# Hybrid decoder block on one core: where early weights are loaded and by whom, when the last row is transposed, and how early the first FFN weights are asked for

## The chip, the core and the metric

The kernel runs on one core of a Trainium2 chip. The core has a matrix engine (TensorE, "PE" in the profile, with its weight loads on the row "PEld"), a vector engine (DVE), a scalar engine (ACT), GpSimd (POOL), and SyncE (SP), which here only issues DMA transfers ("SPq" in the profile; a transfer issued by ACT is "ACTq"). On-chip data lies in SBUF, matmul results in eight PSUM banks, everything else in HBM ("DRAM"). The metric is the device time of one execution in microseconds, measured as a median over runs.

## The reference

One decoder block over x of 2048 tokens by 1024 channels, all in float32:

```
h = rmsnorm(x, g_mix_pre) * (1 + scale_m) + shift_m
q, k, v, u = split(h @ w_in)                      # 8 heads of 64, and 512 pooling channels
mix = concat(stick_breaking_attention(q, k, v), pooling_mixer(u)) @ w_out
x = x + gate_m * rmsnorm(mix, g_mix_post)
h = rmsnorm(x, g_ffn_pre) * (1 + scale_f) + shift_f
f = (silu(h @ w_gate) * (h @ w_up)) @ w_down      # 1024 -> 2816 -> 1024
x = x + gate_f * rmsnorm(f, g_ffn_post)
```

The shifts, scales and gates come from a vector c by a small product. Only the end of the mix and the FFN matter here.

## The kernel before

**Products.** A float32 product is made of three matmuls in a shorter format: each operand is split into a high part (a cast) and a low part (the rest), and hi*hi, hi*lo... are summed in a bank (`mm3`, lines 69 to 71). So whatever enters a product is first split: ACT casts (line 1173) and writes the rounded value into a PSUM bank (line 1180), DVE subtracts (line 1181). `split_by_bank` does this with the banks 6 and 7 in turn ("rounded").

**Fewer products.** The FFN's products are made by a Winograd form of Strassen's scheme: seven half-size products instead of eight, at the price of sums of operands ahead of them and sums of results behind them. For the first quarter of each matrix (`inner`) the scheme is applied once more, inside. POOL makes most operand sums: `p_s` (lines 1338 to 1344) for the inner blocks, `wd` (line 1558) for w_down, `hs` (line 1558) for the tokens, `g_s` and `u_s` (lines 1436 to 1447) for w_gate and w_up.

**The mix loop.** For 16 rows of 128 tokens PE makes the product with w_out (`mix`); `after_mix` squares it (ACT, line 1241), scales it (DVE, line 1245), which frees its bank, and adds the old x, which was loaded as `xr` (SP, line 1236; POOL, line 1247). `ffn_rows` normalizes the new row, and `put_h2` transposes it on PE (`f_pt`, line 134), scales it (`f_h`, lines 139 and 142) and stores it as operand of the FFN (`h2d`). In this loop a scheduler sets the order on every engine.

**The steps.** From the last row on, the order of PE, ACT, DVE and POOL is the written one; SP's order is still the scheduler's, which may put a transfer far ahead of its written place if its buffer is free. The work is a list of steps, one product group each. First come 22 inner blocks (q = 0 and 1, j = 0 to 10, in all m = 11q + j), each of seven steps of six matmuls, named a, e, f, b, h, i and d after their results. Then come the 11 blocks of `gate_up` for the first half of the tokens, whose first is interleaved: g(s2), the last inner block's d, g(s3), g(s1), u(s2), u(s3), u(s1) and so on, twelve matmuls each. Each step has a list `ahead` of actions that are done so many steps sooner: loads, sums. Splits are made up to six steps ahead, sums of results one step behind.

**What hangs on what.** The raw weights of an inner block (`p`, 512 KB in two loads, lines 1318 to 1326) go into one of four tiles, w320 and w321 of the pool `ring` and w320 and w321 of the pool `fx`. `fx` lies where the mix loop has its tiles and opens when the loop closes. The first tiles of gate_up (`g`, `u`, two loads of 512 KB each, line 1416) use the same four. The side tasks are put between the steps: `second_operands` (the last row's transposes and the operands of q = 1), `main_operands` (tokens for gate_up, during q = 1), `rest_operands` (`b_raw`, `t_raw`, split into `b22` and `t4`, at the entry of gate_up). `down_sums` loads four pieces of w_down (`wd`, line 1568), makes four sums on POOL six to nine steps later and stores them (`tdt`, line 1573) for the end of the kernel, 11 groups in all; its four tiles (tag "tr") are the same in each group, so a group's loads wait for the stores of the group before. `px` (line 1513) loads an inner result of 1 MB (`pd`) back for gate_up's sums.

**Banks.** The inner products use the banks 4, 2, 3, 1 and, for d and e, 5 and 0; gate_up's take 4, 2, 3, 0, 1, 5 in turn. So its g(s2) waits until the last inner h has been read from bank 4 (DVE, `u3p`, line 1390), its g(s3) until the last i has been read from bank 2 (DVE, `p_c`, line 1368), its u(s2) until the last d has been read from bank 0.

## Time and profile before

| what | value |
|---|---|
| median of 3 runs | 2243.64 us (2243.42 to 2246.16) |
| the profiled execution's own time | 2245.18 us |
| its span, first to last instruction | 2243.3 us |
| PE busy | 2204.7 us (98%) |
| DVE, ACT, POOL busy | 1604.1, 1352.3, 1301.1 us |
| mean granted PE clock | 0.996 |
| DMA | 478.13 MB, 213 GB/s over the span |

The profile is one execution. A timeline row gives start, duration, engine, line, operation and "output<-inputs"; the bracket at its end is the idle time of that engine just before, with what ended it. A wait row sums such idle times by who waited for whom. A merged row ("x4") starts at its first and lasts to the end of its last instruction. Numbers of buffers are left out of the names there; in the instruction order below they stand.

### The profile page before, as it was taken

Reading aid. Unit: us, or ns where it says so; the run is one execution under the profiler, and the core shown is the slowest. Engines: PE = TensorE matmul, PEld = TensorE weight load, DVE = VectorE, ACT = ScalarE, POOL = GpSimd, SP = SyncE. Lnnn points to the kernel's source line nnn. Section 1 sums busy time; section 2 is a strip of 40 time slices with the busy share of each in tenths; the row PEclk is TensorE's granted clock in tenths of the full one; section 3 lists DMA queues with packets and bytes.
Section 4 is the critical chain, followed back from the end, with each engine's and each line's share of the span. In section 5 each row is a group of like instructions: output and inputs, shape, how many; then the busy total and the mean of one; then the engine's idle time right before and its main releaser. Section 6 shows DMA issues by size and latency. Waiting matters only on the chain. (4 is left out here: it accounts for less than half of the span.)

```text
span 2243.3 us, 34420 instructions
## 1 busy us (share of the span) xinstructions
PE 2204.7 (98%) x10481; PEld 1824.0 (81%) x10481; DVE 1604.1 (72%) x2386; ACT 1352.3 (60%) x2752; POOL 1301.1 (58%) x1702
## 2 busy tenths in 40 slices
PE   8999999999999999999998999999999999999998
PEld 6888888888888887878887888888888888888887
DVE  7874599999999965557786565566877666555566
ACT  6335599898999844457665555545545455544444
POOL 1452277787779955538875777762314888761003
PEclk9999999999999999999999999999999999999999
DMA  9986876533443456668999566558768755548664
GB/s 316 346 280 211 283 203 182 145 109 114 118 123 104 159 177 191 211 225 278 300 336 322 180 199 191 185 190 285 236 219 277 248 192 193 191 147 311 210 189 149
DMA packets 364214, 478.13 MB, mean 213 GB/s; under 512 B 23735, under 2 KB 211707, under 8 KB 361085
## 3 DMA queue, kind: packets, MB, share of 16 engines
q1 hardware_dynamic: 361948, 472.78, 65.8%
q10 hardware_dynamic: 2080, 3.15, 0.5%
q8 instruction: 83, 1.36, 0.3%
q14 instruction: 103, 0.84, 0.1%
HBM read 323.27 MB, written 152.57 MB: 212 GB/s over the span
## 5 line engine op out<-in xcount | busy, mean ns | idle before, releaser
L952 POOL TENSOR_TENSOR w<-sg,pr 128x512 f32<-128x512 f32 (+2 forms) x320 | 306.2, 957 | 46.4 <-DVE pr L947 15.2
L947 DVE TENSOR_TENSOR_SCAN pr<-pr,carry,begin 128x512 f32<-128x512 f32 x192 | 244.0, 1271 | 0.0
L931 ACT ACTIVATE sg<-z 128x512 f32<-128x512 f32 (+2 forms) x320 | 183.8, 574 | 50.9 <-PE z L929 41.5
L60 DVE TENSOR_TENSOR wtl<-wt,wth 128x512 fp32r<-128x512 f32 (+1 forms) x320 | 189.5, 592 | 17.8 <-ACT wth L59 15.6
L59 ACT CAST wth<-wt 128x512 fp32r<-128x512 f32 (+1 forms) x320 | 183.0, 572 | 10.4 <-PE wt L963 8.1
L933 ACT ACTIVATE pr<-z 128x512 f32<-128x512 f32 (+2 forms) x320 | 183.0, 572 | 0.0
L1531 POOL TENSOR_TENSOR s<-s,cu 128x512 f32<-128x512 f32 x88 | 116.1, 1319 | 110.6 <-DVE cu L1530 105.5
L963 PE MATMUL wt<-ident,w 128*128 128x128 f32 x1088 | 172.4, 273 | 1.5 <-POOL pr L943 1.1
L963 PEld LDWEIGHTS wt<-ident,w 128*128 128x128 f32 x1088 | 134.1, 140 | 32.7 <-POOL pr L943 1.9
L1521 ACT ACTIVATE s<-s 128x512 f32<-128x512 f32 x88 | 55.6, 633 | 164.2 <-DVE s L1520 164.2
L978 PE MATMUL av<-wth,vt 128*128 128x512 f32 (+1 forms) x320 | 126.2, 394 | 0.9 <-ACT o L983 0.8
L70 PE MATMUL dn0p<-w0p_l,g0p_h 128*128 128x512 f32 x308 | 120.1, 390 | 1.3 <-DVE w0p_l L60 1.3
L71 PE MATMUL dn0p<-w0p_h,g0p_l 128*128 128x512 f32 x308 | 120.0, 390 | 0.0
L69 PE MATMUL dn0p<-w0p_h,g0p_h 128*128 128x512 f32 x308 | 120.0, 390 | 0.0
L928 PE MATMUL z<-kt,qt 128*128 128x512 f32 (+2 forms) x320 | 118.7, 371 | 0.7 <-ACT pr L933 0.6
L979 PE MATMUL av<-wtl,vt 128*128 128x512 f32 (+1 forms) x320 | 117.9, 369 | 1.3 <-DVE wtl L60 1.2
L929 PE MATMUL z<-kt,qt 128*128 128x512 f32 (+2 forms) x320 | 117.1, 366 | 0.0
L69 PE MATMUL dn1p<-w1p_h,g1p_h 128*128 128x512 f32 x292 | 113.7, 390 | 0.0
L70 PE MATMUL dn1p<-w1p_l,g1p_h 128*128 128x512 f32 x292 | 113.7, 390 | 0.0
L71 PE MATMUL dn1p<-w1p_h,g1p_l 128*128 128x512 f32 x292 | 113.7, 389 | 0.0
L1181 DVE TENSOR_TENSOR u_s_l<-u_s,rounded 128x512 fp32r<-128x512 f32 x63 | 43.3, 688 | 97.7 <-ACT rounded L1180 97.7
L944 DVE TENSOR_TENSOR_SCAN pr<-pr,zero,begin 128x128 f32<-128x128 f32 (+3 forms) x128 | 111.1, 870 | 1.7 <-ACT pr L933 1.7
(774 smaller groups left out, 7180.4 us busy)
## 6 DMA issues: line engine op xcount, KB each, us to landing
pd<-p_c SPq DMA_DIRECT2D x88, 256.0 KB, 4.5
px<-pd SPq DMA_DIRECT2D x22, 1024.0 KB, 5.7
g<-in_w_gate_dram SPq DMA_DIRECT2D x42, 512.0 KB, 4.2
u<-in_w_up_dram SPq DMA_DIRECT2D x42, 512.0 KB, 5.4
wc<-in_w_cond_dram SPq DMA_DIRECT2D x32, 512.0 KB, 7.2
qt<-qd SPq DMA_DIRECT2D x64, 256.0 KB, 4.0
kt<-kd SPq DMA_DIRECT2D x96, 128.0 KB, 3.3
vt<-vd SPq DMA_DIRECT2D x48, 256.0 KB, 3.9
```

What stands on the lines that cost most here:

```text
L59: nc.scalar.copy(hi, src)
L60: low.tensor_tensor(lo, src, raw(hi), ALU.subtract)
L69: nc.tensor.matmul(ps, lh, rh, start=first and i == 0, stop=False)
L70: nc.tensor.matmul(ps, lh, rl, start=False, stop=False)
L71: nc.tensor.matmul(ps, ll, rh, start=False, stop=last and i == n - 1)
L928: nc.tensor.matmul(z[:, 0:L], qt[:, 0, i * P:(i + 1) * P], keys, start=True, stop=False)
L931: nc.scalar.activation(sg[:, 0:L], z[:, 0:L], AF.Sigmoid, scale=0.125)
L933: nc.scalar.activation(pr[:, 0:L], z[:, 0:L], AF.Sigmoid, scale=-0.125)
L947: nc.vector.tensor_tensor_scan(keys, keys, begin, carry, ALU.mult, ALU.bypass)
L952: nc.gpsimd.tensor_tensor(w[:, 0:L], sg[:, 0:L], pr[:, 1:L + 1], ALU.mult)
L963: nc.tensor.transpose(wt[:, i * P:(i + 1) * P], wss[u][i][:, b * P:(b + 1) * P], ident)
L978: nc.tensor.matmul(av[:, lo0:], vb, wh[:, lo0:], start=first, stop=False)
```

## The change

It has six parts.

1. Inner blocks: the four weight tiles are taken in the same rotation, shifted by one block, except for the first. Block 2 is in ring w321 where it was in ring w320, block 3 in fx w320 where it was in ring w321, and so on.
2. The raw weights of the last inner block (m = 21) lie in a tile of the pool of the tokens' operands (tag "y22"), which the 1 MB tile `px_0` takes afterwards.
3. The weight loads of blocks 2 and 5 are issued by ACT, at their place in ACT's written order, instead of SP.
4. Block 0 of gate_up asks for its weights 18 and 16 steps ahead (g before: 16 and 13, u before: 14 and 10), and makes u's sums two steps sooner.
5. The last row's transposes, and the operand work behind them in the same task, come two steps later.
6. The w_down groups stand 12 steps apart instead of 13, the first two steps later (10 + 12i instead of 8 + 13i), the last so eight steps sooner.

```diff
--- before.py
+++ after.py
@@ -1316,14 +1316,17 @@
         st = {}
 
         def load():
-            turn = (2 * HF - 1 - m) % 4
+            turn = 0 if m == 1 else (2 * HF - 2 - m) % 4
             if m == 0:
                 st["g"], st["u"], st["s12"], st["s34"] = (t[:, n] for t in raw_pair(ring, name, (P, 2, TB)) for n in range(2))
             else:
-                w = raw_tile(ring if turn > 1 else fx, turn % 2 == 0, name, (P, 2, TB))
+                if m == 2 * HF - 1:
+                    w = opools["0"].tile([P, 4, TB], F32, tag="y22", bufs=1, name=f"{name}_32")
+                else:
+                    w = raw_tile(ring if turn > 1 else fx, turn % 2 == 0, name, (P, 2, TB))
                 st["g"], st["u"] = w[:, 0], w[:, 1]
             for n, src in (("g", w_gate), ("u", w_up)):
-                nc.sync.dma_start(st[n].rearrange("p (k n) -> p k n", k=HK), rows_of(src, q * HK, j))
+                (nc.scalar if m in (2, 5) else nc.sync).dma_start(st[n].rearrange("p (k n) -> p k n", k=HK), rows_of(src, q * HK, j))
 
         half = TB // 2
         one, two = slice(0, half), slice(half, TB)
@@ -1489,7 +1492,7 @@
             r.insert(0, r.pop(3))
             ahead = ((9, load_a22), (7, load0), (5, load1)) if kind == "g" else ((12, load_a22), (8, load0), (7, load1))
         elif sb == at == 0:
-            ahead = ((16, load0), (13, load1), (8, s3), (7, s2), (6, s1), (5, s4)) if kind == "g" else ((14, load0), (10, load1), (6, s3), (5, s2), (4, s1), (3, s4))
+            ahead = ((18, load0), (16, load1), (8, s3), (7, s2), (6, s1), (5, s4)) if kind == "g" else ((18, load0), (16, load1), (8, s3), (7, s2), (6, s1), (5, s4))
         elif at == 1 and kind == "g":
             ahead = ((10 if sb else 13, load0), (10 if sb else 8, load1), (6, s3), (5, s2), (4, s1), (3, s4))
         else:
@@ -1596,6 +1599,8 @@
         yield
         yield
         nxt = load(0)
+        yield
+        yield
         put_h2(*late.pop(0), fx)
         yield
         yield
@@ -1956,7 +1961,7 @@
         at[rest_operands] = len(r) - 2
         for i in range(HF):
             for n, op in zip((0, 6, 7, 8, 9), down_sums(i)):
-                r[8 + 13 * i + n].ahead.append((0, op))
+                r[10 + 12 * i + n].ahead.append((0, op))
         for sb in range(2):
             for n in range(HF):
                 s = gate_up(sb, (n - 1) % HF if sb else n, n)
```

What it does to the order of instructions is seen at three places. In these rows `p_2_...` is inner block 2 of q = 0, `p_10_...` the last of q = 1, the numbers at the end are buffers.

On SP, in the mix loop, before; xr is the old x of a row, h2d and x1d are stores of earlier rows, m, l the operands of the next products:

```order
L1282 DMA h2d_120<-f_h_11564 128x512
L1058 DMA m_11486<-mtd_98 128x4x128 x2
L1249 DMA x1d_112<-x_8_11573 128x1024
L1056 DMA l_3_11923<-mld_100 128x4x128
L1326 DMA p_2_320_13100<-in_w_gate_dram 128x4x128
L1326 DMA p_2_320_13100<-in_w_up_dram 128x4x128
L1326 DMA p_3_321_13206<-in_w_up_dram 128x4x128
L1236 DMA xr_11676<-in_x_dram 128x1024
L1058 DMA m_11486<-mtd_96 128x4x128
```

and now:

```order
L1282 DMA h2d_120<-f_h_11564 128x512
L1058 DMA m_11486<-mtd_98 128x4x128 x2
L1249 DMA x1d_112<-x_8_11573 128x1024
L1056 DMA l_3_11923<-mld_100 128x4x128
L1236 DMA xr_11676<-in_x_dram 128x1024
L1058 DMA m_11486<-mtd_96 128x4x128
```

The weights of blocks 2 and 3 (and the load of w_gate for block 3 a round earlier) have left the mix loop: block 3's come on SP after the last row of the loop, block 2's on ACT at the start of the steps.

On DVE, at the last row's transposes (f_h from f_pt), before; p_0 and p_1 are the inner blocks 0 and 1:

```order
L1181 TENSOR_TENSOR p_1_s_l<-p_1_s_13097,rounded 128x512
L1368 TENSOR_TENSOR p_0_c_13161<-bp_0_13138,p1p_0_13116 128x512
L142 TENSOR_SCALAR f_h_13172<-f_pt_13167,af,bf 128x128 x4
L1390 TENSOR_TENSOR u3p_0_13199<-hp_0_13154,u2p_0_13145 128x512
L1368 TENSOR_TENSOR p_0_c_13201<-ep_0_13103,u3p_0_13199 128x512
L1368 TENSOR_TENSOR p_0_c_13217<-ip_0_13192,u3p_0_13199 128x512
L1181 TENSOR_TENSOR p_1_s_l<-p_1_s_13118,rounded 128x512
```

and now:

```order
L1181 TENSOR_TENSOR p_1_s_l<-p_1_s_13097,rounded 128x512
L1371 TENSOR_TENSOR p_0_c_13161<-bp_0_13138,p1p_0_13116 128x512
L1393 TENSOR_TENSOR u3p_0_13177<-hp_0_13154,u2p_0_13145 128x512
L1371 TENSOR_TENSOR p_0_c_13179<-ep_0_13103,u3p_0_13177 128x512
L1371 TENSOR_TENSOR p_0_c_13195<-ip_0_13170,u3p_0_13177 128x512
L1181 TENSOR_TENSOR p_1_s_l<-p_1_s_13118,rounded 128x512
L142 TENSOR_SCALAR f_h_13208<-f_pt_13203,af,bf 128x128 x4
```

The transposed row's scaling stands four instructions later; on PE the transposes themselves stood between the products hp and ip of block 0 and now stand behind ip and block 1's ap, ahead of dp.

On POOL, at the entry of gate_up, before; wd is the last group of w_down, g_0 and u_0 the first weights of gate_up:

```order
L1344 TENSOR_TENSOR p_10_s_15526<-p_10_321_15405,p_10_s_15512 128x256
L1558 TENSOR_TENSOR wd_512_15506<-wd_512_15510,wd_512_15506 128x512
L1558 TENSOR_TENSOR wd_0_15504<-wd_512_15506,wd_0_15504 128x512
L1436 TENSOR_TENSOR g_0_s_15619<-g_0_320_15493,g_0_321_15545 128x512
L1558 TENSOR_TENSOR wd_512_15510<-wd_512_15510,wd_0_15504 128x512
L1443 TENSOR_TENSOR g_0_s_15633<-g_0_321_15545,g_0_s_15619 128x512
L1558 TENSOR_TENSOR wd_0_15508<-wd_0_15508,wd_0_15504 128x512
L1439 TENSOR_TENSOR g_0_321_15545<-g_0_321_15545 128x512
L1447 TENSOR_TENSOR g_0_s_15673<-g_0_320_15493,g_0_s_15633 128x512
L1436 TENSOR_TENSOR u_0_s_15718<-u_0_320_15587,u_0_321_15654 128x512
```

and now:

```order
L1561 TENSOR_TENSOR wd_0_15384<-wd_0_15384,wd_0_15380 128x512
L1346 TENSOR_TENSOR p_10_s_15533<-p_10_32_15419 128x256
L1347 TENSOR_TENSOR p_10_s_15533<-p_10_32_15419,p_10_s_15517 128x256
L1439 TENSOR_TENSOR g_0_s_15627<-g_0_320_15476,g_0_321_15505 128x512
L1446 TENSOR_TENSOR g_0_s_15640<-g_0_321_15505,g_0_s_15627 128x512
L1442 TENSOR_TENSOR g_0_321_15505<-g_0_321_15505 128x512
L1450 TENSOR_TENSOR g_0_s_15675<-g_0_320_15476,g_0_s_15640 128x512
L1439 TENSOR_TENSOR u_0_s_15693<-u_0_320_15536,u_0_321_15572 128x512
```

The four w_down sums stand ahead of the last of block 21's own sums, and the eight sums of gate_up's block 0 follow each other.

On SP at the same place, before; pd are stores of inner results (`p_8_c`: block 19, `p_9_c`: block 20):

```order
L1416 DMA g_0_321_15545<-in_w_gate_dram 128x8x128
L1364 DMA pd_165<-p_8_c_15524 128x512
L1364 DMA pd_164<-p_8_c_15537 128x512
L1513 DMA px_0_15617<-pd_164 128x2048
L1416 DMA u_0_320_15587<-in_w_up_dram 128x8x128
L1364 DMA pd_165<-p_8_c_15571 128x512
```

and now, in two pieces:

```order
L1419 DMA g_0_321_15505<-in_w_gate_dram 128x8x128
L1576 DMA tdt_168<-wd_512_15382 128x512
L1419 DMA u_0_320_15536<-in_w_up_dram 128x8x128
L1576 DMA tdt_167<-wd_0_15380 128x512
L1367 DMA pd_164<-p_8_c_15514 128x512
L1576 DMA tdt_166<-wd_512_15386 128x512
L1367 DMA pd_165<-p_8_c_15530 128x512
L1419 DMA u_0_321_15572<-in_w_up_dram 128x8x128
```

```order
L1419 DMA g_1_320_15723<-in_w_gate_dram 128x8x128
L1516 DMA px_0_15625<-pd_164 128x2048
L1367 DMA pd_165<-p_9_c_15685 128x512
L1659 DMA b_raw<-h2d_124 128x512
L1659 DMA b_raw<-h2d_125 128x512
```

`px_0` stood between the loads of g and u, and u's second load eight rows further down, behind three results of block 20 (`p_9_c`); now u's second load stands ahead of all of these, and `px_0` comes after them and ahead of `b_raw`.

## The prediction

> **What bounds the kernel now.** The page's first part comes first, then who waited for whom on PE from the end of the attention on, then timelines at those waits.
>
> ```profile
> PE 2204.7 (98%) x10481; PEld 1824.0 (81%) x10481; DVE 1604.1 (72%) x2386; ACT 1352.3 (60%) x2752; POOL 1301.1 (58%) x1702
> ...
> PE mix L69 <- DVE x L1245: 5.6, 4, 2.9
> PE t_g L69 <- DVE p_c L1368: 3.8, 1, 3.8
> PE t_g L69 <- DVE u3p L1390: 2.8, 1, 2.8
> PE f_pt L134 <- DVE x1s L1263: 1.9, 1, 1.9
> ...
> PE ep L69 <- ACT rounded L1180: 0.3, 1, 0.3
> ```
>
> PE is the bound: 2204.7 of 2243.3 us. The change removes no matmul, so all it can give is in PE's waits, and these are few: 5.6 us in the mix loop (four times), 1.9 + 1.0 at the last row's transposes, 2.8 + 3.8 at the entry of gate_up, 0.3 between. All lie before 1224 us; behind that the change moves nothing that PE waits for. A wait costs more than itself where the clock falls: the transposes' and the entry's rows below show products at half speed.
>
> **Part 1: weight loads leave the mix loop.** SP's timeline, the chain from its load of the old x to PE's wait of 2.9, and the landing times of all 15 such loads:
>
> ```profile
> 847.69 0.46 SPq L1326 DMA_DIRECT2D p<-in_w_gate_dram  x1
> 848.20 1.05 SPq L1326 DMA_DIRECT2D p<-in_w_up_dram  x2
> 849.35 0.44 SPq L1236 DMA_DIRECT2D xr<-in_x_dram  x1
> ...
> 856.46 1.30 POOL L1247 TENSOR_TENSOR x<-x,xr 128x512 f32<-128x512 f32 x1 [5.24 <-DMA xr<-in_x_dram]
> ...
> 860.28 1.06 ACT L1255 ACTIVATE xr<-x 128x1024 f32<-128x1024 f32 x1 [9.41 <-POOL x L1247]
> ...
> 866.48 1.41 DVE L1245 SCALAR_TENSOR_TENSOR x<-mix,mr_r,gm 128x512 f32<-128x512 f32 x2 [0.44 <-POOL mr_r L125]
> ...
> DMA to landing us min/median/max: 3.6/4.6/7.1
> ```
>
> Three weight loads (768 KB) are issued right ahead of xr. It starts 1.66 us later for it (849.35 - 847.69) and lands 7.1 us after issue by POOL's start (856.46 - 849.35), where xr's median is 4.6. POOL has stood 5.24 us; ACT's squares come behind it, and the next bank is released 10.0 us later (866.48 - 856.46). Without the three loads xr starts at 847.7 and lands at 852.3: 4.1 us sooner. The 2.9 us wait then vanishes. The three later ones (5.6 - 2.9 = 2.7) are of rows whose rounds carry operand sums as well; they were held by a chain that was late by the 2.9 us PE had waited, so 4.1 - 2.9 = 1.2 us is their cover, spent once. I let 2.2 stay in all: **gain 3.4**. Bounds: 2.0 (xr is as late without these loads, only the 1.66 of issue and a bit saved) and 5.6. At their new places the loads meet DMA engines that are 84% busy (last row of the next fence). Block 2's are issued 12 steps of 1.36 us ahead of its first product, 16.3 us; its sums and splits take some 5 of these, and 11 remain against 7.1 for the slowest xr. So I set nothing for it.
>
> The issue by ACT I price at nothing too: four issues of about 0.46 us each (the SP row of p) leave SP and stand among ACT's casts, and ACT is busy for 60% of the span. The Trainium skill ("DMA: Bandwidth & Descriptors", section "Issuing engines are not separate DMA queues") says that transfers started by different engines run on the same 16 engines, so that only issue time is saved; by it ACT's part is worth at most 4 x 0.46 = 1.8 us of SP, and the sum is unchanged. No run here shows it yet.
>
> **Part 2: the transposes two steps later.** PE, ACT and DVE around them, and two stretches with the granted clock, the DMA share and GB/s at the end:
>
> ```profile
> 996.32 0.39 PE L71 MATMUL hp<-v32p1h,p_s_l 128*128 128x512 f32 x1
> 998.66 1.01 PE L134 MATMUL f_pt<-ident,x1s 128*128 128x128 f32 x4 [1.95 <-DVE x1s L1263]
> 1000.67 1.11 PE L134 MATMUL f_pt<-ident,x1s 128*128 128x128 f32 x4 [1.00 <-DVE p_s_l L1181]
> ...
> 1003.29 0.63 PE L70 MATMUL ip<-v14p1l,p_u_h 128*128 128x512 f32 x1
> 1003.72 0.63 PE L71 MATMUL ip<-v14p1h,p_u_l 128*128 128x512 f32 x1
> ...
> 1006.22 0.40 PE L69 MATMUL dp<-y22p,p_s_h 128*128 128x512 f32 x1
> ...
> 997.01 0.58 ACT L1373 COPY p1p<-ap 128x512 f32<-128x512 f32 x1
> ...
> 998.53 0.68 DVE L1382 TENSOR_TENSOR u2p<-fp,p1p 128x512 f32<-128x512 f32 x1
> 999.93 0.69 DVE L1181 TENSOR_TENSOR p_s_l<-p_s,rounded 128x512 fp32r<-128x512 f32 x1 [0.73 <-POOL p_s L1344]
> ...
> 868.00:918.00 50.00, 47.32 (x224) 39.00 (x223) 27.81 (x61) 24.69 (x58) 27.58 (x30) 1.00 0.61 188
> ...
> 994.00:1007.00 13.00, 10.05 (x36) 7.71 (x36) 8.15 (x15) 8.15 (x17) 7.54 (x10) 0.74 0.84 273
> ```
>
> hp's last matmul starts at 996.32, so the next could at 996.55; dp starts at 1006.22. Between stand ip and ap, twelve matmuls of 0.227 (hp to dp's own pitch), 2.72 us, and eight transposes, some 1.0: 5.9 us are lost, 2.95 in waits and the rest to the clock (0.43 from one ip matmul to the next; granted 0.74). Now ip comes first, but not at once: its bank is free when p1p has been copied from it (997.6), ap's when u2p is done (999.2). ip starts at 997.75, ap at 999.35 and ends at 1000.7. The first four transposes need the bank that p_s_l (999.93, to 1000.62) reads, the next four that of the second p_s_l, which by DVE's new order stands behind p_c, u3p, p_c and p_c of about 0.6 each: 1000.6 + 4 x 0.6 = 3.0, with its own 0.69 to 1003.7. Then four transposes, and dp at 1004.4: 1.8 sooner. The price of a step is so not the wait on x1s that goes (1.95), since p1p, u2p and p_s_l are next in line. Against it, PE stands 1.2 us before ip and 2.4 behind the first four transposes, in place of 1.95 and 1.0, and may again be clocked down, up to 1.7 us (a stretch of 3.4 us at half pitch holds eight matmuls of 0.43, each 0.2 too long, as at 1217 to 1221 below). The 2.9 us wait of the mix loop cost no clock (granted 1.00 from 868 on), the 1.95 here did, so I take half of the 1.7: **gain 1.0**, bounds -0.5 and +3.
>
> The Trainium skill ("TensorE: Matmul & The Clock Gate", section "Part 1: The HAM clock gate") has the clock set by a free-running window of some 3.4 us, halved after an idle one; the trace agrees as far as half speed there starts and ends 6.8 us apart (998.8 to 1005.6). By this rule a wait cannot be judged by its length alone, and this term is 1.8 if the window ends inside the wait and 0.1 if it holds the whole of it.
>
> **Part 3: the entry of gate_up.** PE, DVE, POOL and SP there, and two stretches (DMA share and GB/s are the last two numbers):
>
> ```profile
> 1208.38 0.47 PE L69 MATMUL t_g<-t2h,g_s_h 128*128 128x512 f32 x1 [2.81 <-DVE u3p L1390]
> 1216.50 0.47 PE L69 MATMUL t_g<-t3h,g_s_h 128*128 128x512 f32 x1 [3.78 <-DVE p_c L1368]
> ...
> 1218.54 0.63 PE L69 MATMUL t_g<-t3h,g_s_h 128*128 128x512 f32 x1
> ...
> 1198.77 0.42 DVE L1181 TENSOR_TENSOR p_u_l<-p,rounded 128x256 fp32r<-128x256 f32 x1 [0.78 <-ACT rounded L1180]
> ...
> 1203.83 0.69 DVE L1181 TENSOR_TENSOR g_s_l<-g_s,rounded 128x512 fp32r<-128x512 f32 x1 [3.80 <-ACT rounded L1180]
> ...
> 1207.55 0.68 DVE L1390 TENSOR_TENSOR u3p<-hp,u2p 128x512 f32<-128x512 f32 x1
> ...
> 1215.07 0.69 DVE L1181 TENSOR_TENSOR u_s_l<-u_s,rounded 128x512 fp32r<-128x512 f32 x1 [6.11 <-ACT rounded L1180]
> 1215.67 0.69 DVE L1368 TENSOR_TENSOR p_c<-ip,u3p 128x512 f32<-128x512 f32 x1
> ...
> 1196.04 2.67 POOL L1558 TENSOR_TENSOR wd<-wd,wd 128x512 f32<-128x512 f32 x2 [6.98 <-DMA wd<-in_w_down_dram]
> 1198.66 1.29 POOL L1436 TENSOR_TENSOR g_s<-g,g 128x512 f32<-128x512 f32 x1
> ...
> 1211.06 1.29 POOL L1436 TENSOR_TENSOR u_s<-u,u 128x512 f32<-128x512 f32 x1 [4.86 <-DMA u<-in_w_up_dram]
> ...
> 1203.96 0.84 SPq L1416 DMA_DIRECT2D u<-in_w_up_dram  x1
> ...
> 1177.00:1187.00 10.00, 10.00 (x46) 8.29 (x45) 8.57 (x15) 4.99 (x10) 8.67 (x10) 1.00 0.71 247
> 1187.00:1200.00 13.00, 13.00 (x59) 10.74 (x59) 8.89 (x15) 6.03 (x12) 5.94 (x7) 1.00 1.03 349
> ```
>
> Both waits are queues. u3p, which frees bank 4, stands on DVE behind splits of g_s; these wait for POOL, which stood 6.98 us for w_down and then put wd sums between g's. p_c, which frees bank 2, stands behind a split of u_s; POOL began that sum at 1211.06, when u's second load, issued only at 1203.96, had landed (7.1 us). Behind it eight matmuls last 0.63 in place of 0.39 and add 8 x 0.2 = 1.6, slow restarts 0.4: 2.8 + 3.8 + 1.6 + 0.4, about **8.6 to 8.8**.
>
> Now the last w_down group is asked for eight steps, 10.9 us, sooner, in the stretch where the DMA engines are only 71% busy: the 29% left of 10 us, at 349 GB/s, is its 1 MB. POOL's eight sums follow each other. By the new order SP issues, from the w_down loads (near 1177) to u's second load, 1 MB of w_down, 0.5 of block 21, 2 of gate_up and ten stores of 256 KB: 6 MB, 17 us at 349 GB/s, so that it lands near 1194 to 1197, 14 us sooner. g's sums (four of 1.29) end near 1199, u's near 1203; DVE can split the first u_s by 1203.5, while p_c is due at 1209.5 (PE had ended ip by 1205.6, 1208.38 - 2.81; g(s2) takes 2.72, d 1.36). u3p then waits for hp alone: 0.3 to 0.5 stay. **Gain 8.3**, bounds 4.0 (the second wait halved, the first kept) and 8.8.
>
> What is late next: `px_0` shares its tile with block 21's weights, so SP stands at it until DVE has split the last of them (p_u_l, to 1199.2), and `b_raw` and `t_raw` behind it on SP. px_0's 1 MB and b_raw's 1 MB take 2.9 us each at that rate: px_0 near 1204.5, b_raw by 1208 to 1209. DVE's queue then runs b22l, u2g, s and the last split of u ahead of the p_c that frees bank 0 for u(s2). By the durations I get 1214.3, and u(s2) is due at 1215.1. The cover is 0.8 us.
>
> **Part 4: denser w_down groups.** Ten intervals are 12 steps instead of 13, 1.36 us less each, with the same work. POOL and DMA see 8% more of it until 1190. Its risk is a rival below; the 0.3 us wait at ep may go or come again: 0, bounds -0.5 and +0.5.
>
> **Sum.** 3.4 + 1.0 + 8.3 = 12.7. The profiled execution took 2245.18 us, 1.9 outside its span and 1.5 above the median of 2243.64; it would take 2232.5, and the median 2230.9. **Forecast: 2231 us.** With all lower bounds (2.0 - 0.5 + 4.0 - 0.5 = 5.0) it is 2238.6, with all upper ones (5.6 + 3.0 + 8.8 + 0.5 = 17.9) 2225.7.
>
> **Rivals.**
>
> *px_0 and b_raw take over the wait.* They need only be 3 us later than worked out to use up the 0.8 us and stop PE for 2.2, with a clocked-down stretch of 1.6: 2231 + 3.8 = **2235**. For it: u took 7.1 us to land, g and b_raw stand in the same full queue (share 1.03). Against it: b_raw is issued some 6 us sooner than before. Chance 0.17.
>
> *The mix loop and the transposes give nothing.* The chain of the mix loop is as long with its operand sums, and the 2.4 us gap at the transposes costs a half-speed stretch: 2243.6 - 8.3 = **2235.3**. For it: three of the four waits in the loop have no weight loads ahead. Chance 0.11.
>
> *The entry stays.* The scheduler places transfers by its own estimate, and SP may stand at a result of the inner blocks (pd) ahead of u's second load as it does now; then only 4.4 are gained: **2239.2**, at the edge of what counts as no change. Against it: the new row order has that load behind block 19's results, not block 20's. Chance 0.10.
>
> *Slower: POOL stands for w_down in every group.* A group's loads wait for the stores of the one before, and 1.36 us of the time between is gone. POOL takes its sums in order:
>
> ```profile
> 1104.97 4.04 POOL L1558 TENSOR_TENSOR wd<-wd,wd 128x512 f32<-128x512 f32 x3 [3.73 <-DMA wd<-in_w_down_dram]
> ...
> 1122.32 0.47 PE L69 MATMUL ep<-v14p2h,p_s_h 128*128 128x512 f32 x1 [0.32 <-ACT rounded L1180]
> ```
>
> Here it stood 3.73 us for w_down and p_s came late behind it, so that PE waited 0.32 seventeen us on. If each of ten groups lands 1.36 later against its sums and PE pays it, that is 13.6, the last one keeps the entry as it is, and 3.4 + 1.0 remain: 2243.6 + 13.6 - 4.4 = **2252.8**. It decides as soon as POOL's stand passes some 4 us in every group, since 3.73 was the first that PE felt. Against it: 0.3 us is all that PE paid in ten groups. Chance 0.10.
>
> **How the numbers follow.** The forecast's case, from 2226 to 2234, has 0.52. A run of this kernel tells apart 0.2%, 4.5 us. Faster are the forecast and the first two rivals, 0.52 + 0.17 + 0.11 = 0.80; the same is the entry that stays, 0.10; slower the last, 0.10. The range of 8 in 10 takes in the forecast and the rivals near 2235 and stops at the edge of the entry's case: 2226 to 2239.
>
> **What would show it.** Right: no weight load ahead of xr on SP in the mix loop, POOL's idle before its x under 2 us, and PE's waits for DVE's x under 3 us in all; ip directly behind hp, and dp within 8 us of hp's end; u's second load on SP ahead of block 20's results, POOL's g and u sums without a gap above 2 us, and no t_g wait above 1 us. Wrong: a wait of t_u for DVE's last p_c, with b22l behind DMA b_raw in DVE's queue (first rival); POOL idle at wd above 4 us in several groups and new waits of inner products on ACT or DVE (last rival).

## The result, and the profile after

| | before | changed |
|---|---|---|
| median | 2245.33 us (2243.42 to 2247.3, 8 runs) | 2238.53 us (2236.15 to 2242.75, 8 runs) |
| ratio to before | | 0.9971 (95% interval 0.996 to 0.9982) |
| a second set of runs, ratio | | 0.9966 (0.9952 to 0.998) |
| profiled execution, span | 2243.3 us | 2234.3 us |

The change makes the kernel faster by 6.5 to 8 us. The forecast was 12.7, so the sign was right and the size was not. What PE waits for in the changed kernel, from the end of the attention on (time in all, times, longest):

```profile
PE f_pt L134 <- DVE p_s_l L1181: 2.5, 1, 2.5
PE ap L69 <- DVE u2p L1385: 2.1, 1, 2.1
PE t_u L69 <- DVE p_c L1371: 1.4, 1, 1.4
PE ip L69 <- ACT p1p L1376: 1.0, 1, 1.0
PE dn0p L70 <- DVE w0p_l L60: 0.9, 1, 0.9
PE ep L69 <- ACT p1p L1376: 0.9, 1, 0.9
PE mix L69 <- DVE x L1245: 0.7, 2, 0.4
PE ep L69 <- DVE p_c L1371: 0.7, 1, 0.7
```

The mix loop's waits fell from 5.6 to 0.7 us and both t_g waits (2.8 and 3.8) are gone. But among the inner blocks, where one ep had waited 0.3 us before, ap and ep now wait 2.1, 0.9 and 0.7, and t_u waits 1.4. The kernel was profiled a second time; from the starts of the same matmuls in each profile against those of before, the time gained comes out so:

| place (us in the profile before) | forecast | first profile | second profile |
|---|---|---|---|
| mix loop, 794 to 894 | 3.4 | 5.3 | 5.4 |
| last row's transposes, to 1008 | 1.0 | 0.4 | 0.5 |
| inner blocks, 1008 to 1130 | 0 | 0.6 | 0.6 |
| inner blocks, 1130 to 1180 | 0 | -4.4 | -8.4 |
| entry of gate_up: t_g | 8.3 | 8.5 | 8.6 |
| entry of gate_up: t_u | 0 | -1.4 | 0.3 |
| the rest, ahead of 794 and behind 1224 | 0 | 0.0 | -1.8 |
| sum, from the spans | 12.7 | 9.0 | 5.1 |

Three of the four terms lie within their bounds. What is missing is the loss between 1130 and 1180 us, and it is not the same in two executions of one program. In the first profile it looks so on PE, DVE and POOL:

```profile
1174.08 0.47 PE L69 MATMUL ap<-yap2h,p_g_h 128*128 128x512 f32 x1 [2.13 <-DVE u2p L1385]
...
1172.64 0.69 DVE L1181 TENSOR_TENSOR t3l<-hs,rounded 128x512 fp32r<-128x512 f32 x1 [4.54 <-ACT rounded L1180]
1173.25 0.68 DVE L1385 TENSOR_TENSOR u2p<-fp,p1p 128x512 f32<-128x512 f32 x1
...
1162.63 1.30 POOL L1561 TENSOR_TENSOR wd<-wd,wd 128x512 f32<-128x512 f32 x1 [3.48 <-DMA wd<-in_w_down_dram]
...
1168.74 1.28 POOL L1561 TENSOR_TENSOR wd<-wd,wd 128x512 f32<-128x512 f32 x1
1169.99 1.28 POOL L1561 TENSOR_TENSOR hs<-hs,hs 128x512 f32<-128x512 f32 x1
1171.23 1.27 POOL L1561 TENSOR_TENSOR wd<-wd,wd 128x512 f32<-128x512 f32 x1
```

Read backwards: ap waits for a bank that u2p frees; u2p stands on DVE behind t3l, the split of a token sum; t3l waits for hs, which POOL made at 1169.99, between two sums of w_down. Ahead of these POOL had stood 3.48 us for w_down's load. Whether the sums or the load is the cause is what the experiments ask.

The mix loop, the same rows as before (SP, then the chain's end on POOL):

```profile
846.32 0.36 SPq L1056 DMA_DIRECT2D l<-mld  x1
846.73 0.50 SPq L1236 DMA_DIRECT2D xr<-in_x_dram  x1
...
851.48 1.28 POOL L1247 TENSOR_TENSOR x<-x,xr 128x512 f32<-128x512 f32 x1 [1.17 <-DMA m<-mtd]
...
862.37 1.29 POOL L1247 TENSOR_TENSOR x<-x,xr 128x512 f32<-128x512 f32 x1 [0.92 <-DVE x L1245]
```

No weight load stands ahead of xr, and it starts 2.6 us sooner (849.35 before). POOL's x comes at 851.48 instead of 856.46 and no longer waits for xr, and the x of the next row comes at 862.37 instead of 867.37. At the transposes the new order gives:

```profile
992.68 0.50 PE L69 MATMUL ip<-v14p1h,p_u_h 128*128 128x512 f32 x1 [1.00 <-ACT p1p L1376]
...
998.83 1.12 PE L134 MATMUL f_pt<-ident,x1s 128*128 128x128 f32 x4 [2.46 <-DVE p_s_l L1181]
999.60 0.78 PE L69 MATMUL dp<-y22p,p_s_h 128*128 128x512 f32 x1
1000.17 0.63 PE L70 MATMUL dp<-y22p,p_s_h 128*128 128x512 f32 x1
```

ip is 1.0 late and the second four transposes 2.5, as worked out; dp follows at half speed.

### The profile page after: what moved, and what is told of

Read it like the earlier page. It is cut to its first block, busy times and chain, and to the rows that moved or that the text cites. A ratio compares the mean times of both kernels' runs of the same rounds, so it can differ in the third digit from the quotient of the medians.

```text
span 2234.3 us, 34412 instructions
## 1 busy us (share of the span) xinstructions
PE 2201.7 (99%) x10481; PEld 1820.6 (81%) x10481; DVE 1604.3 (72%) x2386; ACT 1353.1 (61%) x2752; POOL 1300.4 (58%) x1702
## 4 chain that ended last, share of the span: by engine, by line
PE 54%; POOL 1%; DVE 1%; DMA 1%; issue 1%; ACT 1%; SPq 0%; DVEq 0%; ACTq 0%; POOLq 0%
PE t_u L69 4%; PE t_u L70 4%; PE t_u L71 4%; PE t_g L70 3%; PE t_g L69 3%; PE t_g L71 3%; PE dn0p L70 3%; PE dn0p L69 3%; PE dn0p L71 3%; PE dn1p L69 3%; PE dn1p L71 3%; PE dn1p L70 3%; PE mix L69 1%; PE mix L70 1%; PE mix L71 1%
```

## The experiments

Each kernel was timed beside the kernel before. Theory A: w_down's groups share POOL with the tokens' sums, and where both fall into the same steps the latter come late, DVE stands at their splits, and PE at the banks behind them. In its first form it puts this down to POOL's stand for w_down's loads, later to the time of w_down's sums. Where an expectation sets other theories beside it, it says what each would show.

**w_down 13 steps apart again.** `r[10 + 12 * i + n]` becomes `r[8 + 13 * i + n]`.

> The changed kernel with the w_down groups 13 steps apart again (8 + 13i), all else as changed. Theory A (the denser groups make POOL stand for w_down's loads, the tokens' sums hs come late behind it, and DVE stands at their splits): the three new waits of PE between 1155 and 1178 us (0.7 + 2.1 + 0.9, some 4.2 with slow restarts) go, under 0.7 us stays there. At the entry of gate_up POOL takes w_down's sums between g's again, so of the 8.4 us gained there 2 to 5 come back. Time within 2 us of the changed kernel's 2238.5. Rival B (these waits come from the operand task two steps later or from the weights' new places): the three waits stay within 1 us of what they were, and only the entry loses, 2241 to 2244.

Measured: 2240.31 us, ratio 0.9982 (0.9973 to 0.999). Between 1120 and 1185 us PE waits for nothing at all; the one wait behind it is at the entry, with POOL ahead of it:

```profile
PE t_g L69 <- DVE u3p L1393: 5.8, 1, 5.8
...
1194.68 2.64 POOL L1561 TENSOR_TENSOR wd<-wd,wd 128x512 f32<-128x512 f32 x2 [9.53 <-DMA wd<-in_w_down_dram]
1197.29 1.29 POOL L1439 TENSOR_TENSOR g_s<-g,g 128x512 f32<-128x512 f32 x1
1198.54 1.28 POOL L1561 TENSOR_TENSOR wd<-wd,wd 128x512 f32<-128x512 f32 x1
```

The waits inside came with the spacing, as theory A has it. All the profiles bear this out: in the seven of kernels with full sums 12 steps apart PE waits 2.9 to 5.7 us in the inner blocks behind 1010 us, in the six new ones of kernels with 8 + 13i (one of them with its first group at 10) not at all, and in the three with 10 + 13i 0.9 to 2.6 us. So it is not only how dense the groups are that counts, but also on which steps they fall. The spacing is also what clears the entry, where POOL now stands 9.53 us for the last group. Twelve steps give in one place and take in the other.

**The transposes at their old steps.** The two new `yield`s are taken out.

> The changed kernel with the last row's transposes and the operands behind them at their old steps. Theory A: the region of the transposes alone changes; it gains 0.4 us in the changed kernel's profile (dp 1.6 sooner, half speed takes 1.2), so the time is 2238.5 to 2240.5 and the waits between 1155 and 1178 us stay within 1 us. Rival B (the operand task two steps later makes those waits): they go, and the time is 2234 to 2236.

Measured: 2237.84 us, 0.9966 (0.9954 to 0.9978). No difference from the changed kernel can be told, and the inner waits stay (1.9, 1.5 and 0.9); the time lies just below theory A's range and above the rival's. So moving the transposes by two steps is worth nothing that can be measured, and the operands behind them do not cause the waits.

**Blocks 2 and 5 loaded by SP.** `(nc.scalar if m in (2, 5) else nc.sync)` becomes `nc.sync`.

> The changed kernel with the loads of blocks 2 and 5 issued by SP instead of ACT, the buffers as changed. Theory A (what hurts is weight loads that stand ahead of xr on SP in the mix loop; whoever has an open buffer gets there, and these two have one): the row loads xr stand behind three weight loads again, PE's waits for DVE's x are 4.5 to 6 us instead of 0.7, time 2242.5 to 2244.5. Rival B (the new rotation of the buffers is enough): waits under 2 us, time within 1.5 us of 2238.5.

Measured: 2242.9 us, 0.9992 (0.9983 to 1.0). SP and the sum of the loop's waits:

```profile
848.01 0.50 SPq L1329 DMA_DIRECT2D p<-in_w_up_dram  x1
848.63 0.43 SPq L1329 DMA_DIRECT2D p<-in_w_gate_dram  x1
849.10 0.51 SPq L1329 DMA_DIRECT2D p<-in_w_up_dram  x1
849.72 0.44 SPq L1236 DMA_DIRECT2D xr<-in_x_dram  x1
...
PE mix L69 <- DVE x L1245: 3.7, 3, 2.4
```

As in the kernel before, three weight loads stand ahead of xr, now those of blocks 2 and 5, whose buffers are open in the loop. The waits are 3.7, below the 4.5 to 6 expected, but a stretch at half speed follows the longest, and from the matmuls' starts the loop gains 0.5 us instead of 5.3. So the rotation alone does not help; the loads from SP went to where their buffers were open, and those from ACT stayed where they were written (block 2's went out at 989.78).

**gate_up's first loads at their old steps.** The line of `ahead` for block 0 as before: g 16 and 13, u 14 and 10, u's sums at 6, 5, 4, 3.

> The changed kernel with gate_up block 0's loads and sums at their old steps (g 16 and 13, u 14 and 10 ahead; u's sums two steps later). Theory A (the entry's gain comes from the last w_down group, which has left SP and POOL there; the loads would come in time anyway): the two waits of t_g (2.8 + 3.8 before, none now) stay under 1.5 us in all, time within 2 us of 2238.5. Rival B (asking for the weights sooner is the gain): 4 us or more of t_g waits return, time 2243 or more.

Measured: 2236.14 us, 0.9963 (0.9951 to 0.9976); no t_g wait, t_u 0.8. The time is 0.4 us below the range expected. Asking sooner is worth nothing: the entry was cleared by other parts.

**The changed kernel again.**

> The changed kernel itself once more, for a second profile and more times. If its first profile (2236.15 us, the fastest of its eight runs) was a lucky draw of where half speed falls, its waits of PE are the same within 1 us in all and its granted clock is lower; median 2237 to 2240. If the waits themselves differ from run to run, the three between 1155 and 1178 us (3.7 in all) change by more than 1.5 us.

Measured: 2236.88 us (5 runs). The expectation's first branch was wrong: its waits between 1130 and 1182 are not those of the first profile.

```profile
PE ep L69 <- DVE p_c L1371: 4.0, 2, 3.0
...
PE ap L69 <- DVE u2p L1385: 0.9, 1, 0.9
...
PE ep L69 <- ACT p1p L1376: 0.8, 1, 0.8
```

They are 5.7 us in all instead of 3.7, and eight slow matmuls follow the 3.0. The loss there differs from run to run.

**w_down's sums left out in three groups.** In `down_sums`, for j in 7, 8 and 9, the loaded pieces are handed on without `combine`; these sums are left out.

> The changed kernel with POOL's twelve sums of the w_down groups 7, 8 and 9 left out: the loaded pieces are stored as they are, so loads and stores stay and the output's w_down part is that of other weights. Theory A1 (POOL's time: sums of w_down between the tokens' sums put the latter late): no PE wait over 0.7 us between 1120 and 1185 us, where the changed kernel has 3.7 and 5.7 in its two profiles; time 2231 to 2234. Theory A2 (the transfers: POOL only stands for w_down's late loads): waits of 2.5 us or more stay there, since without the sums the loads are as late as before, time over 2235.

Measured: 2231.42 us, 0.9941 (0.9926 to 0.9956). A stretch of 82 us, first of the second profile of the changed kernel, then of this one (busy PE, PEld, DVE, ACT, POOL; clock, DMA share, GB/s; in the first profile PE was busy for 78.34):

```profile
1100.00:1182.00 82.00, 76.28 (x326) 61.75 (x325) 58.41 (x95) 48.90 (x92) 64.02 (x65) 0.98 0.95 318
```

```profile
1100.00:1182.00 82.00, 82.00 (x364) 67.89 (x363) 66.34 (x107) 54.15 (x101) 55.09 (x59) 1.00 0.99 340
...
POOL p_s L1341 <- DMA p<-in_w_up_dram: 15.2, 5, 8.0
POOL hs L1561 <- DMA hs<-h2d: 5.7, 2, 3.0
POOL wd L1561 <- DMA wd<-in_w_down_dram: 4.4, 2, 3.4
```

PE is busy for all of it, though the loads and stores are as before and the DMA engines at 0.99. So w_down's sums on POOL are what makes PE wait, and the traffic is not. But this run takes two things away: the sums' own time (twelve of 1.30 us) and, with them, POOL's stand for those groups' loads. The next two runs part them.

**The stand kept, the time gone.** In the same three groups each sum is made over 8 of its 512 columns, `tensor_tensor(t[:, 0:8], x[:, 0:8], y[:, 0:8], op)`.

> The changed kernel, with w_down's sums of groups 7, 8 and 9 made over 8 of their 512 columns (the other 504 columns of these sums are left out). Each sum still stands for its load at its place on POOL, so POOL's waits for the loads stay and its 1.3 us each (12 sums, 15 us) go. If the sums' time is what makes the tokens' sums late, PE waits between 1120 and 1182 us are under 0.5 us, and the time is near 2231 to 2234, as without the sums. If POOL's stand for w_down's loads is what does it, 3 to 6 us of waits stay between 1120 and 1182 and the time is 2236 to 2239.

Measured: 2232.19 us, 0.9944 (0.9931 to 0.9956). PE waits for nothing between 1100 and 1185 us, though POOL stands 11.0 us for w_down's loads (7.4 in the changed kernel's first profile):

```profile
POOL wd L1576 <- DMA wd<-in_w_down_dram: 8.1, 2, 5.8
POOL hs L1561 <- DMA hs<-h2d: 6.7, 2, 4.0
POOL wd L1561 <- DMA wd<-in_w_down_dram: 2.9, 1, 2.9
```

**The time kept, the stand gone.** Each of those sums becomes three additions of a 128x128 tile that nothing else uses.

> The changed kernel, with each of w_down's sums of groups 7, 8 and 9 replaced by three additions of a 128x128 tile that nothing else uses (these twelve sums are left out; the loaded pieces are stored as they are). POOL is busy at the same places for about as long (three of 0.4 to 0.5 us for one of 1.3, from 0.74 for a 128x256), and stands for no load there. If the sums' time makes the tokens' sums late, 2 to 6 us of PE's waits stay between 1120 and 1182 us and the time is 2236 to 2239. If the stand for the loads does it, waits there are under 0.5 us and the time is 2231 to 2234. If it takes both, this and the kernel with short sums each show under 1 us of waits.

Measured: 2232.11 us, 0.9942 (0.9929 to 0.9956). POOL's groups and PE's only wait in the stretch:

```profile
L1579 POOL TENSOR_TENSOR idle<-idle 128x128 f32<-128x128 f32 x36 | 14.4, 400 | 2.1
...
PE ep L69 <- DVE p_c L1373: 0.9, 1, 0.9
```

The twelve additions take 14.4 us where the sums took 15.6, and 0.9 of the 3.7 and 5.7 us of waits is left. So neither the sums' time nor the stand for the loads does most of it alone: a POOL that spends 14.4 us there on additions is in time but for 0.9 us if it need not stand, and a POOL that stands 11 us is in time if the sums cost little. Theory A had named the stand in its first form and the sums' time in its later one, never both. One thing these runs do not part: SP stands less in them at the stores of w_down's sums, and the tokens' loads are issued on the same queue. From 1100 to 1182 us SP waits there 14.7 us for POOL's `wd` in the changed kernel, 6.7 with the short sums, 2.2 with the additions beside, and 11.5 with the groups 13 steps apart. Against it as the cause, POOL stands longer for the tokens' loads with the short sums (6.7 us) than in the changed kernel (4.0), and PE still waits for nothing.

**The last group behind the entry.** Ten groups at 8 + 13i, the eleventh in block 3 of gate_up:

```diff
-                r[10 + 12 * i + n].ahead.append((0, op))
+                if i < HF - 1:
+                    r[8 + 13 * i + n].ahead.append((0, op))
...
+                if not sb and n == 3:
+                    for k, op in zip((0, 6, 7, 8, 9), down_sums(HF - 1)):
+                        r[len(r) - 10 + k].ahead.append((0, op))
```

> The changed kernel with the first ten w_down groups 13 steps apart again (8 + 13i) and the last group moved behind the entry, to block 3 of gate_up. Theory A (w_down's sums hurt where they stand among the tokens' sums on POOL, 1155 to 1178, and the last group where it stands among gate_up's, 1205 to 1220): both places are free, no wait over 0.7 us between 1010 and 1230 us, 5 to 6 us less than the changed kernel: 2232 to 2234.5. Rival B (12 steps apart is needed to free the entry): t_g waits 3 us or more, 2238 or more. Rival C (the group is only a wait moved): a new wait of 2 us or more between 1230 and 1300 us.

Measured: 2234.97 us, 0.9951 (0.9938 to 0.9963). No wait between 1010 and 1205 us, no t_g wait at the entry and no new one between 1230 and 1300, as theory A expected, and not as its rivals did. The time is 0.5 us above the range expected and 1.9 us below the changed kernel's beside it, which the intervals do not part. But theory A allowed no wait over 0.7 us up to 1230, and t_u waits 2.6, more than in the changed kernel's profiles (1.4 and 0):

```profile
1201.66 1.29 DVE L60 TENSOR_TENSOR b22l<-b_raw,b22h 128x512 fp32r<-128x512 f32 x2
1205.97 0.69 DVE L1454 TENSOR_TENSOR u2g<-t_g,px 128x512 f32<-128x512 f32 x1 [3.03 <-DMA px<-pd]
```

DVE stands 3.03 us for px_0, and the p_c that frees t_u's bank stands behind it.

**b_raw and t_raw three steps sooner** (in that kernel; their splits stay in place).

> The kernel with the last group in block 3 of gate_up (ten groups 13 apart), with the loads of b_raw and t_raw asked for three steps sooner (their splits stay in place), so that three of the four b_raw loads stand ahead of px_0 on SP. Theory: the t_u wait of 2.6 us comes from ACT standing for b_raw behind px_0's 1 MB, so it falls under 0.8, time 2231.5 to 2233.5 against 2235.0. Rival (bank 0 is late by DVE's work alone): the wait stays over 1.5.

Measured: 2236.61 us, t_u 3.9. The expectation failed: DVE still stands 3.63 us for px_0 itself. The edit moved little, since three of the four b_raw loads stood ahead of px_0 without it too (the first two at 1187.56, now at 1187.74), and b_raw was in time in both (b22l at 1201.66 and 1201.29). In the kernel below that joins later transposes with the last group behind the entry it made no difference either:

> Transposes four steps later, ten groups at 10 + 13i, the last in block 3 of gate_up, b_raw and t_raw three steps sooner. That kernel without the last part had no t_u wait in its profile, so at most 1 us is to be had: 2230 to 2232.5.

Measured: 2232.31 us, against 2231.89 for the kernel without this part.

**px_0 in two halves.** Block 21's weights lie in the second and fourth quarter of px_0's tile; the first and third quarter, which g wants, are loaded without waiting for them, the others at the third g step. First in the kernel with the last group behind the entry:

> The kernel with the last w_down group in block 3 of gate_up (ten groups 13 apart, t_u wait 2.6 us), with block 21's weights in the second and fourth quarter of px_0's tile and px_0 loaded in two halves: the first and third quarter, which g wants, without waiting for block 21, the others at the third g step. Theory (the shared tile makes px_0 and what stands behind it late): the t_u wait falls under 0.8 us, 2.5 us less, 2231.5 to 2233.5. Rival (DVE's and ACT's own work): the wait stays over 1.8.

Measured: 2230.94 us, 0.9945 (0.9931 to 0.9958), t_u 0.6. On DVE:

```profile
1201.51 1.29 DVE L60 TENSOR_TENSOR b22l<-b_raw,b22h 128x512 fp32r<-128x512 f32 x2
1202.71 0.68 DVE L1454 TENSOR_TENSOR u2g<-t_g,px 128x512 f32<-128x512 f32 x1
```

u2g follows b22l without a wait. The first half is asked for at 1187.68, the whole was at 1196.60. So the t_u wait is the price of the shared tile, as far as this run shows it: that DVE now also waits for half the bytes only was not tested apart. The time is 0.6 us below the range expected, but the ratio shows less: 0.9945 against 0.9951 without the halves, with intervals that overlap. In the changed kernel:

> The same two halves of px_0 in the changed kernel, all else as changed. Theory: no t_u wait over 0.8 us (1.4 and 0 in the two profiles so far), the waits between 1120 and 1185 us stay (3.7 and 5.7); 2235.5 to 2238.

Measured: 2235.85 us, 0.9964 (0.9952 to 0.9977): no t_u wait, and 4.6 us of inner waits stay, as expected.

**The weight loads alone.** The kernel before with parts 1 to 3 only.

> The kernel before with only the inner blocks' weight loads changed (parts 1 to 3: rotation, block 21's tile, blocks 2 and 5 on ACT). Theory: the mix loop's waits fall from 5.6 to 0.7 us and the rest is as before: 4 to 5.5 us less than before, 2239.5 to 2241.5. At the entry px_0 now waits for block 21's tile; by the theory that part 4 and 6 alone mend the entry, its t_g waits stay 6 us or more. Rival (the late weights cost elsewhere what the loop gains): 2243 or more.

Measured: 2241.85 us, 0.9982 (0.9973 to 0.9991). The time is 0.35 us above the range expected, and the loop's waits are 0.7, as expected. At the entry:

```profile
PE t_u L69 <- DVE p_c L1371: 4.2, 1, 4.2
PE t_g L69 <- DVE u3p L1393: 2.7, 1, 2.7
...
1191.74 0.42 SPq L1419 DMA_DIRECT2D u<-in_w_up_dram  x1
```

Here the expectation was wrong in a useful way. The second t_g wait (3.8 before) is gone without parts 4 and 6: u's second load is issued at 1191.74 instead of 1203.96. Before, block 21's weights lay in the tile that u's second load takes, and it had to wait for their last split (to 1199.2); in the new tile they are out of its way. But px_0 has them in its way now, and t_u's 4.2 takes the gain back.

**The transposes four steps later.** Two more `yield`s, so that they stand behind e of block 1.

> The changed kernel with the transposes and the operands behind them four steps later than before instead of two (behind e of block 1). Theory: the transposes wait for the two banks that the splits use, the second of which DVE frees at the end of four results of block 0; two products more ahead of them cover the 2.5 us wait, and no half speed follows: 1.5 to 3.5 us less than the changed kernel, 2235 to 2237. Rival (the bank is late by PE's own work, so the wait moves along): a wait of 1.5 us or more stays at f_pt or at the next product, time within 1 us of 2238.5.

Measured: 2234.76 us, 0.2 below the range expected, 0.9952 (0.994 to 0.9965). The 2.5 us wait becomes 0.4 and 0.5 and no half speed follows; from the matmuls' starts the place gains 2.7 more than in the changed kernel. In the time, 0.9952 against 0.9966 for the changed kernel beside it, the intervals overlap; the trace shows the gain, the timing alone would not.

**Together.** Transposes four steps later, groups at 10 + 13i, the last behind the entry:

> Both: transposes four steps later, ten w_down groups at 10 + 13i, the last in block 3 of gate_up. By the two theories the gains add: 7 to 9 us less than the changed kernel, 2229.5 to 2232. If one of them is wrong, its part is missing: 2233 to 2236.

Measured: 2231.89 us, 0.9941 (0.9928 to 0.9953); then with px_0 in halves:

> The same two halves of px_0 in the kernel with the transposes four steps later and ten groups at 10 + 13i. That one had no t_u wait in its profile; 2230 to 2232.5.

Measured: 2230.11 us, 0.9938 (0.9925 to 0.995). Left in the inner blocks were waits of 1.4 and 0.9, at 1132.7 and 1136.5 us. With nine of the groups two steps sooner (10, then 8 + 13i from the second on):

> Transposes four steps later, px_0 in two halves, w_down groups at 10 and from the second on at 8 + 13i, the last in block 3 of gate_up. Theory (only the phase of w_down's sums against the tokens' matters): no wait over 0.7 us between 1120 and 1185 us, where 10 + 13i has 1.4 + 0.9; 2226.5 to 2229.5 against 2230.1. Rival (the waits come with the later transposes and operands): 2 us of waits stay near 1130, time within 1 us of 2230.1.

Measured: **2228.26 us** (2226.98 to 2229.18), 0.992 (0.9906 to 0.9933), faster than the kernel before and the changed kernel; from the one just above, the intervals do not part it. Between 1010 and 1230 us one wait is left:

```profile
PE t_u L69 <- DVE p_c L1371: 0.4, 1, 0.4
```

The waits near 1135 went with the shift of two steps, in one profile of each kernel.

## Why the prediction was right and wrong

**Part 1, right, undersized.** The loads ahead of xr were the cause, and ACT's issue is what keeps them out (with SP issuing, the loop gains 0.5 us instead of 5.3). Forecast 3.4, measured 5.3, near the upper bound of 5.6: I let 2.2 of the three later waits stay, and 0.7 stayed. The size that was off is the "4.1 us sooner": xr started 2.6 us sooner, not 1.66, since SP itself came to it 0.9 us earlier, and POOL's x came 5.0 us sooner. With 5.0 the cover behind the 2.9 us wait is 2.1 instead of 1.2, and 0.6 of the 2.7 should stay, about what did. "ACT's issue at nothing" was wrong as a reading of the parts: its transfers cost nothing, but without it the term is almost gone. The sentence of the Trainium skill cited there ("DMA: Bandwidth & Descriptors", section "Issuing engines are not separate DMA queues") counts only issue time as saved. Here what counted is that an ACT transfer keeps its written place.

**Part 2, right in its steps, small in sum.** ip 1.0 late (1.2 forecast), the second transposes 2.46 (2.4), dp 1.6 sooner (1.8). Half speed then took 1.2 of it (0.85 set): 0.4 to 0.5 against 1.0, and no difference in the times. Whether half speed follows differs from profile to profile: of the twelve profiles with the transposes at these steps, all with the same wait of 2.4 to 2.5, eight gain 0.3 to 0.5 there at half speed, and four gain 1.8 to 1.9 at full speed. These are near the two cases, 0.1 and 1.8, that the prediction set apart for this term. With the transposes at their old steps (the run with the two `yield`s out, and the weight loads alone) the place gains 0.6 to 0.7, so the 0.4 to 0.5 are not shown to come from the move.

**Part 3, the size right, the reason partly wrong.** 8.5 and 8.6 against 8.3. But I put u's late load down to its place on SP and to being asked for late; undoing the new asks cost nothing. It was its tile, held by block 21's weights (the weight loads alone brought it to 1191.74), and, for the first wait, the last w_down group on POOL. The overlooked term is thus part 2 of the change, which I had costed only as px_0's risk. That risk was named (cover 0.8 us, b_raw and px_0 behind block 21's split), and it came in about this size: 1.4 and 0 in the changed kernel, 2.6 and 4.2 in others.

**Part 4, wrong, and it is the step that failed.** "Ten intervals are 12 steps ... 0, bounds -0.5 and +0.5": it cost 4.4 and 8.4 us in two profiles. The mechanism stood among the rivals, read from the 0.32 us wait at 1122 (POOL's order puts p_s late), but I priced it as all ten groups or nothing, and let POOL's stand for w_down's loads decide, from 4 us in every group. In the changed kernel's first profile that stand was 3.5 us at most from 1100 to 1182, and the waits came. The runs show that the stand alone does not decide: with POOL standing 11 us for those loads but the sums made short, no wait is left, and with the sums' time kept and no stand, 0.9. It takes both, POOL's own time and its stand, where a group of w_down meets the tokens' sums. The seven profiles at 12 steps lose 3.7 to 8.4 us from the inner blocks' matmuls there, the six new ones at 8 + 13i none; that the groups meet the tokens' sums more often at 12 steps is what the rows at 1162 to 1175 suggest and no run counts. I had not laid the two sets of steps beside each other, and the bound of 0.5 had nothing behind it but 8% more work.

**Range and chances.** 2238.53 lies within 2226 to 2239, and faster had 0.80. The time fell between the case near 2235 and the entry that stays, through a loss that none of the cases had at its size. That it lies inside the range is in part luck: part 4 fell far below its bound, and the 2 us that part 1 gave above its term made up for some of it. Of the second profile's -1.8 outside the four places, 1.2 lies behind 1224 us, where the prediction let the change move nothing; the runs do not show why.

## What to carry to other kernels

A task that is spread evenly over many steps is not to be costed by its engine's mean load: lay its steps beside those of every other task on the engine, since two chains that meet in the same steps make the one with a reader late. When a transfer is late, look first at who still holds its tile and then at the place where it is asked for; and when a tile is given to two users to free another, the second user's wait is the price, which loading in parts can avoid. A transfer on a queue that a scheduler orders goes wherever its buffer opens; to keep it out of a stretch, close the buffer or issue it from an engine whose order is written.

## What the runs showed of the hardware

Whether a wait of PE is followed by half speed did not go by its length. In one kernel 2.64 us at t_u were followed by matmuls of 0.39, in another 2.13 us at t_g by eight slow ones, six of them of 0.63:

```profile
1211.79 0.47 PE L69 MATMUL t_u<-t2h,u_s_h 128*128 128x512 f32 x1 [2.64 <-DVE p_c L1371]
1212.10 0.39 PE L70 MATMUL t_u<-t2l,u_s_h 128*128 128x512 f32 x1
```

```profile
1743.33 0.77 PE L69 MATMUL t_g<-t3h,g_s_h 128*128 128x512 f32 x1 [2.13 <-DVE cu L1533]
1743.90 0.63 PE L70 MATMUL t_g<-t3l,g_s_h 128*128 128x512 f32 x1
```

The first is of the kernel with the last group behind the entry, the second of the one that joins later transposes, the last group behind the entry and b_raw sooner. The same wait in the same place shows it too. At the last row's transposes the changed kernel's dp followed a wait of 2.46 at 0.63 (rows above); with the short sums it follows the same wait at full speed:

```profile
1000.40 0.65 PE L134 MATMUL f_pt<-ident,x1s 128*128 128x128 f32 x4 [2.46 <-DVE p_s_l L1181]
1001.13 0.39 PE L70 MATMUL dp<-y22p,p_s_h 128*128 128x512 f32 x1
```

The Trainium skill ("TensorE: Matmul & The Clock Gate", section "Part 1: The HAM clock gate") has the clock set by a window of some 3.4 us that runs by itself. With that it agrees that the length of a wait alone does not decide. The Trainium skill also says there that the clock falls after at least one idle window of that length, and with that the traces do not agree: waits of 2.13 and 2.46 us are shorter, and half speed followed them.

The same program's waits in a stretch with the DMA engines at 0.95 to 0.97 differed by 2 us between two executions (3.7 and 5.7), so that one profile is not enough to cost a loss there.
